# Attention on 8-column query tiles, its projections spread over four heads, and the keys' copies issued on ScalarE's queue

## The chip, the cores and the metric

One NeuronCore of one Trainium2 chip runs the whole program. TensorE (PE in the profile; its weight loads are PEld) multiplies into PSUM, VectorE (DVE) and ScalarE (ACT) do the elementwise work, GpSimd (POOL) casts some weights, and SyncE (SP) issues most DMAs. The metric is the device time of one execution in microseconds; lower is better. The time before is the median of three runs, 2376.87 us (2376.11 to 2376.95).

## The reference, cut to what matters

Two token streams, a prompt of 1024 tokens on a grid of 16 rows by 64 columns and a sample of 256 tokens on 4 by 64, go through two layers with the same weights. The change touches layer 0 alone: RMSNorm, four projections, attention in a clamped window of 8 rows by 16 columns with a learned bias, a gate, an output projection and the residual.

```python
proj = h @ w_in
q, k, v, g = jnp.split(proj, 4, axis=-1)
q = grid(q) * (NA_HEAD_DIM ** -0.5)
# per query row r: key rows rs..rs+7, key columns in a window of 16
s = jnp.einsum('bjqhd,bijkhd->bhjqik', q_r, k_s).astype(jnp.float32)
s = jnp.where(mask, s + bias, NEG_INF)
p = jax.nn.softmax(...)
o = jnp.einsum('bhjqik,bijkhd->bjqhd', p, v_s)
return (o * jax.nn.silu(g)) @ w_out
```

There are 16 heads of 64 channels. Everything is float32.

## The kernel before

Activations lie channel-major, 128 channels by 1280 tokens (1024 of the prompt, then 256 of the sample), and the prompt's tokens are sorted by grid column, so 128 tokens are 8 columns of 16 rows. Each projection is exact to float32 by three products of a high and a low part in fp32r: `proj` (line 1108) makes channel-major outputs in blocks of 512, 512 and 256 tokens, 24 matmuls a block; `proj_tokens` (line 1124) makes token-major strips of 128 tokens for V, 24 matmuls of 256 columns a strip.

Layer 0 runs over 16 heads. `qk_head(h)` projects queries and keys of a head, splits the keys into KH and KL and copies both from partitions 64 to 127 to partitions 0 to 63 by a DMA on SyncE's queue (lines 202 and 203). `g_pair(p)` makes the gate of two heads, `v_quad(q)` the values of four. `attention(h)` is a Python generator: each `yield n` says that n columns of projection should be streamed before it goes on, and the `Side` object steps it from `tick`, which every projection matmul calls. So the attention of head h is interleaved with the projections for later heads: `qk_head(h + 1)` beside every head, and in addition a whole `g_pair` beside every odd head and a whole `v_quad` beside every fourth. What is left of a head's attention at the end of this is drained. The framework's scheduler then sets the final order on each engine from this order of writing and the dependencies.

A head's prompt has four query tiles j of 16 columns. For a tile, two score blocks (`scores`, one for query rows 0 to 7, one for 8 to 15) of 128 queries by 384 keys: 12 key rows by a slab of 32 columns. Each is two matmuls (KH, then KL; lines 279 and 280), a sum with the bias and a minimum (line 224), Exp (line 225), a reciprocal and a scaling (lines 226 and 227) into a buffer P of 32 by 16 keys whose four unused rows hold zeros. `pv` then turns P with 8 TensorE transposes a tile (line 238), splits the turned block into ph and pl (ScalarE line 241, VectorE line 242) and multiplies both with the four strips of V that the slab covers, in 8 matmuls of 256 columns (line 254) into one PSUM tile O. Lines 259 to 261 take O out with the gate. The sample is a fifth tile: two score blocks of 256 keys (lines 299 and 300), 4 transposes, 4 products. The biases of a head come in three DMAs of 384 KB and one for the sample.

Q is stored with a permuted column order, so that the 128 queries of a score block lie together.

Of the kernel before, what the change touches and what calls it, by code (L numbers as in the profile page):

```python
# [19 lines left out]
NEG = -1e30  # L20
SLAB = [0, 8, 24, 32]
ROWS = [(0, 12), (4, 12)]
# [14 lines left out]
def layer0(ctx, tc, a, h1_out):  # L37
# [77 lines left out]
    def v_quad(q, side):  # L115
        nonlocal wv
        wv = load_v(tc, a, q)
        V = {}
        for s in range(10):
            side.until(lambda: done[4 * q - 1] > (0, 1, 1, 2, 3, 3, 3, 3, 4, 4)[s])  # L120
            V[s] = v_strip(s, token_major(s, side))
        return V

# [51 lines left out]
    with st:  # L175
# [5 lines left out]
        def qk_head(h, side=None):  # L181
# [4 lines left out]
            for b, (t0, n) in enumerate(BLK):  # L186
# [5 lines left out]
                if t0 < NP:  # L192
                    qv = Q[:, :NP].rearrange("p (g c r) -> p c g r", g=2, r=8)[:, t0 // 16:t0 // 16 + 32]
                    tq = t.rearrange("p (c g r) -> p c g r", g=2, r=8)
                else:
                    qv, tq = Q[:, c], t[:, :n]
                nc.scalar.activation(qv[0:64], tq[0:64], AF.Copy)
                nc.scalar.activation(KH[64:128, c], t[64:128, :n], AF.Copy, scale=0.125)
                nc.vector.tensor_sub(qv[64:128], tq[0:64], qv[0:64])
                nc.vector.scalar_tensor_tensor(KL[64:128, c], t[64:128, :n], 0.125, KH[64:128, c],  # L200
                                               op0=OP.mult, op1=OP.subtract)
            nc.sync.dma_start(KH[0:64, :].bitcast(F32), KH[64:128, :].bitcast(F32))
            nc.sync.dma_start(KL[0:64, :].bitcast(F32), KL[64:128, :].bitcast(F32))
            return Q, KH, KL

        def g_pair(p, side=None):
            wh, wl = load_w(tc, a, a["w_g"][p])
            G = []
            for b, (t0, n) in enumerate(BLK):
# [3 lines left out]
                proj(nc, ps, wh, wl, XH, XL, b, side)  # L213
                t = ap.tile([128, 512], F32, name="t", bufs=2)[:, :n]
                nc.vector.tensor_mul(t, ps, rb[:, t0:t0 + n])
                G.append(ap.tile([128, n], F32, name=f"G{b}"))
                nc.scalar.activation(G[b], t, AF.Tanh, scale=0.5)
                nc.vector.scalar_tensor_tensor(G[b], G[b], 1.0, t, op0=OP.add, op1=OP.mult)
            return G
# [9 lines left out]
        def pv(strips, hh, Od, Gv, t1v):  # L229

            O = ps_o.tile([128, 256], F32, name="O")
            ns = len(strips)

            def turned(s0):
                pt = ps_t.tile([128, 2, 256], F32, name="pt")
                for u in range(2):
                    for g in range(2):
                        nc.tensor.transpose(pt[:, u, 128 * g:128 * g + 128], strips[s0 + u][1][g], ident)  # L238
                ph = ap.tile([128, 2, 256], F32R, name="ph", bufs=2)
                pl = ap.tile([128, 2, 256], F32R, name="pl", bufs=2)  # L240
                nc.scalar.activation(ph, pt, AF.Copy)  # L241
                nc.vector.tensor_sub(pl, pt, ph)
                return ph, pl

            ts = []
            for s0 in range(0, ns, 2):
                ts.append(turned(s0))
                yield 800
            for s0 in range(0, ns, 2):
                ph, pl = ts[s0 // 2]  # L250
                for i, p in enumerate((ph, pl)):
                    for u in range(2):
                        v = strips[s0 + u][0][:, hh, :, :].rearrange("p a b -> p (a b)")
                        nc.tensor.matmul(O, v, p[:, u, :], start=(s0 + u + i == 0), stop=(s0 + u + i == ns))  # L254
                    yield 800
            b = 64 * (hh % 2)
            cc = 64 - b
            t1 = ap.tile([128, 256], F32, name="t1", bufs=2)
            nc.scalar.activation(t1[b:b + 64], O[cc:cc + 64], AF.Copy, scale=0.5)
            nc.vector.scalar_tensor_tensor(t1[b:b + 64], O[b:b + 64], 0.5, t1[b:b + 64], op0=OP.mult, op1=OP.add)  # L260
            nc.vector.tensor_mul(Od[b:b + 64], t1v(t1)[b:b + 64], Gv[b:b + 64])

        def attention(h, qkk, V, G, O):
            Q, KH, KL = qkk
            g3 = lambda t: t[:, :NP].rearrange("p (c r) -> p c r", r=16)
            g4 = lambda t, j: t[:, 256 * j:256 * j + 256].rearrange("p (c g r) -> p g c r", g=2, r=8)
            bts = {}

            def scores(j):
                if j != 2:  # L270
                    bts[j] = ap.tile([128, 768], F32, name="bias", bufs=2)
                    nc.sync.dma_start(bts[j], a["bias_p"][h, (0, 1, 1, 2)[j]])
                bt = bts[1 if j == 2 else j]
                s0 = SLAB[j]
                Pt = []
                for g, (r0, nr) in enumerate(ROWS):
                    S = ps_s.tile([128, 512], F32, name="S")[:, :nr * 32]
                    q = Q[:, 512 * g + 128 * j:512 * g + 128 * j + 128]
                    nc.tensor.matmul(S, q, g3(KH)[:, s0:s0 + 32, r0:r0 + nr], start=True, stop=False)
                    nc.tensor.matmul(S, q, g3(KL)[:, s0:s0 + 32, r0:r0 + nr], start=False, stop=True)  # L280
                    p = P[g][j % 2]
                    b = bt[:, 384 * g:384 * g + 384]
                    cr = lambda v: v.rearrange("p (c r) -> p c r", c=32)
                    softmax(cr(S), cr(b), p[:, :, r0:r0 + nr])
                    Pt.append(p)
# [1071 lines left out]
```

## Time and profile before

| what | value |
|---|---|
| median of three runs | 2376.87 us |
| the profiled execution's own time | 2384.96 us |
| its span, first to last instruction | 2383.2 us |
| mean granted TensorE clock | 0.971 |
| stretch of the heads' attention | about 57 to 707 us of the span |
| busy share of the span: PE, DVE, ACT, POOL | 95%, 70%, 51%, 23% |

Start times in the trace count from the span's first instruction. A matmul's duration there includes the time that it stands in the pipeline, so that two matmuls overlap: what one costs TensorE is the distance from its start to the start of the next one. The view by stretches gives the busy time of each engine and the count of its instructions between two moments; the granted clock in it is 1.00 at full speed.

### The profile page before, as it was taken

The numbers are of one execution on the slowest core, as the hardware profiler recorded it, in microseconds if no ns is written. First come the engines' busy times: TensorE is split into PE (matmuls) and PEld (weight loads), VectorE is DVE, ScalarE is ACT, GpSimd is POOL, SyncE is SP. The second block draws the span as 40 slices with busy tenths as digits, with TensorE's granted clock in tenths as the row PEclk, the third lists the DMA queues.
The fourth block names the chain that finished last, engine by engine and source line by source line (L and its number), as shares of the span: only waits on it lengthen the run. The fifth ranks groups of instructions, "written<-read, shape, count | busy, mean of one in ns | idle before, by whom it ended". The sixth has DMA issues, their size and how long they took to land.

```text
span 2383.2 us, 37349 instructions
## 1 busy us (share of the span) xinstructions
PE 2267.1 (95%) x13462; PEld 1967.4 (83%) x13462; DVE 1676.6 (70%) x3888; ACT 1213.0 (51%) x2742; POOL 544.1 (23%) x636
## 2 busy tenths in 40 slices
PE   8999999999999789999999999999999889999998
PEld 7889889889778678888989889898777777777887
DVE  5675774883783758578697786977588888886444
ACT  6553553563572543433444434443677777765233
POOL 2000101000120422222232222322544444420000
PEclk9999999999999899889999999998999999999999
DMA  5453443543556243333444433543533334347332
GB/s 173 119 125 86 118 119 92 130 106 97 139 164 197 67 108 102 77 102 108 112 115 115 129 99 112 115 116 103 135 95 110 115 108 114 105 152 249 105 105 86
DMA packets 150329, 281.34 MB, mean 118 GB/s; under 512 B 45824, under 2 KB 82688, under 8 KB 150144
## 3 DMA queue, kind: packets, MB, share of 16 engines
q1 hardware_dynamic: 137760, 233.86, 32.0%
q0 software_dynamic: 12384, 45.09, 10.6%
q8 instruction: 106, 1.74, 0.3%
q14 instruction: 79, 0.65, 0.1%
HBM read 203.54 MB, written 64.88 MB: 113 GB/s over the span
## 4 chain that ended last, share of the span: by engine, by line
PE 66%; DVE 21%; ACT 4%; DMA 4%; issue 4%; POOL 1%; SPq 0%; DVEq 0%; ACTq 0%; POOLq 0%
PE mm L1108 29%; PE mm L1124 11%; DVE acc L447 3%; PE O L254 3%; DVE tmp L562 3%; DVE X L564 3%; PE k L873 2%; PE k L864 2%; PE o L884 2%; PE pt L238 2%; PE u L839 2%; PE o L839 2%; PE m L610 1%; PE m L953 1%; PE S L280 1%
## 5 line engine op out<-in xcount | busy, mean ns | idle before, releaser
L1108 PE MATMUL mm<-xh,wh 128*128 128x512 f32 (+1 forms) x1536 | 556.7, 363 | 6.6 <-ACT wh L1060 5.9
L1108 PE MATMUL mm<-xh,wl 128*128 128x512 f32 (+1 forms) x1536 | 554.4, 361 | 6.4 <-DMA wl<-w_qkv 3.5
L1108 PE MATMUL mm<-xl,wh 128*128 128x512 f32 (+1 forms) x1536 | 559.7, 364 | 0.0
L1108 PEld LDWEIGHTS mm<-xh,wh 128*128 128x128 f32 x1536 | 293.0, 191 | 38.4 <-ACT wh L1060 6.4
L1108 PEld LDWEIGHTS mm<-xh,wl 128*128 128x128 f32 x1536 | 292.8, 191 | 37.9 <-DMA wl<-w_qkv 3.7
L1108 PEld LDWEIGHTS mm<-xl,wh 128*128 128x128 f32 x1536 | 293.1, 191 | 29.8 <-issue 0.5
L1124 PE MATMUL mm<-wh,xh 128*128 128x256 f32 x960 | 283.8, 296 | 5.1 <-DVE z L473 4.4
L1124 PE MATMUL mm<-wl,xh 128*128 128x256 f32 x960 | 284.0, 296 | 2.4 <-DMA wl<-w_z 1.9
L1124 PE MATMUL mm<-wh,xl 128*128 128x256 f32 x960 | 282.4, 294 | 0.3 <-POOL xl L66 0.3
L447 DVE SCALAR_TENSOR_TENSOR acc<-raw,cw,acc 128x1282 f32<-128x1282 f32 x128 | 201.1, 1571 | 46.8 <-ACT acc L445 45.1
L1124 PEld LDWEIGHTS mm<-wh,xh 128*128 128x128 f32 x960 | 188.9, 197 | 9.8 <-DVE z L473 4.8
L1124 PEld LDWEIGHTS mm<-wl,xh 128*128 128x128 f32 x960 | 188.9, 197 | 6.0 <-DMA wl<-w_z 2.2
L1124 PEld LDWEIGHTS mm<-wh,xl 128*128 128x128 f32 x960 | 189.0, 197 | 3.7 <-issue 2.0
L1060 ACT ACTIVATE wh<-wraw 128x1024 fp32r<-128x1024 f32 x94 | 98.8, 1056 | 141.9 <-PE mm L1108 81.0
L1058 POOL CAST wh<-wraw 128x1024 fp32r<-128x1024 f32 x30 | 31.4, 1048 | 471.5 <-PE mm L1108 373.2
L1108 PE MATMUL mm<-yh,wh 128*128 128x512 f32 (+1 forms) x384 | 135.7, 356 | 1.7 <-ACT yh L982 1.7
L1108 PE MATMUL mm<-yl,wh 128*128 128x512 f32 (+1 forms) x384 | 137.0, 358 | 0.1
L1108 PE MATMUL mm<-yh,wl 128*128 128x512 f32 (+1 forms) x384 | 136.4, 357 | 0.6 <-DVE wl L1062 0.6
L860 POOL TENSOR_TENSOR Al<-A,Ah 128x128 fp32r<-128x128 f32 x160 | 76.2, 482 | 174.2 <-ACT Ah L859 146.8
L1064 ACT ACTIVATE wl<-wraw 128x1024 fp32r<-128x1024 f32 x86 | 90.8, 1055 | 31.7 <-PE mm L1108 11.4
L450 ACT ACTIVATE th<-acc 128x1282 f32<-128x1282 f32 x32 | 40.9, 1277 | 129.3 <-DVE acc L447 129.3
L241 ACT ACTIVATE ph<-pt 128x512 fp32r<-128x512 f32 x144 | 84.3, 593 | 32.2 <-PE pt L238 31.3
(324 smaller groups left out, 5303.0 us busy)
## 6 DMA issues: line engine op xcount, KB each, us to landing
bias<-bias_p SPq DMA_DIRECT2D x48, 384.0 KB, 3.1
wraw<-w_qkv SPq DMA_DIRECT2D x32, 512.0 KB, 4.3
wl<-w_qkv POOLq DMA_DIRECT2D x32, 512.0 KB, 7.5
qkv_spill<-th SPq DMA_DIRECT2D x32, 512.0 KB, 2.6
wraw<-w_go SPq DMA_DIRECT2D x32, 512.0 KB, 3.7
z_spill<-z SPq DMA_DIRECT2D x80, 128.0 KB, 1.7
z<-z_spill SPq DMA_DIRECT2D x80, 128.0 KB, 2.1
wraw<-w_qk SPq DMA_DIRECT2D x16, 512.0 KB, 5.6
```

The costliest lines, as they stand in the source:

```text
L238: nc.tensor.transpose(pt[:, u, 128 * g:128 * g + 128], strips[s0 + u][1][g], ident)
L241: nc.scalar.activation(ph, pt, AF.Copy)
L254: nc.tensor.matmul(O, v, p[:, u, :], start=(s0 + u + i == 0), stop=(s0 + u + i == ns))
L447: nc.vector.scalar_tensor_tensor(acc, r[:, i:i + m], cw[:, f, i:i + 1], acc, op0=OP.mult, op1=OP.add)
L562: nc.vector.tensor_mul(tv, N[:, 0:c, c:c + 1].to_broadcast([128, c, n]), X[:, c:c + 1, c + 1:32].to_broadcast([128, c, n]))
L564: nc.vector.tensor_add(X[:, 0:c, c + 1:32], X[:, 0:c, c + 1:32], tv)
L839: self.tc.nc.tensor.matmul(ps, w[x], v[y], start=(first and i == 0), stop=(i == 2))
L860: nc.gpsimd.tensor_sub(As[d][1], A[:, d, c], As[d][0])
L1060: nc.scalar.activation(wh, raw, AF.Copy)
L1064: nc.scalar.activation(wl, raw, AF.Copy, scale=-1.0)
L1108: nc.tensor.matmul(ps, w[:, k, :], x[k][b], start=(k == 0 and i == 0), stop=(k == KD - 1 and i == 2))
L1124: nc.tensor.matmul(ps, x[k][b][:, cc], w[:, k % 4, :], start=(k == 0 and i == 0), stop=(k == KD - 1 and i == 2))
```

## The change

The query tile is now read as two blocks m of 8 columns by all 16 rows, which is how the tokens lie already. A block needs the keys of its own 8 columns and of the 8 on each side: three strips of 128 keys, two at the left and the right end of the grid (blocks 0 and 7). Scores are again 128 by 384, or 128 by 256 for the two end blocks, over plain slices. Two blocks still share one output tile: the two strips in the middle serve both of them (256 columns), the outer ones one each (an "edge", 128 columns). A first turned block holds the two middle strips, a second one the edges. The transposes for tile j now follow the products of tile j-1, instead of preceding the products of the same tile at once. All prompt biases of a head come in one DMA of 448 KB.

The gate's blocks and the strips of V are handed out in pieces: heads 0, 4, 8, ... get block 2 of the gate, six strips and `qk_head`, heads 1, 5, ... block 0 of the next gate and `qk_head`, heads 2, 6, ... blocks 1 and 2 and `qk_head`, heads 3, 7, ... two blocks of the next gate, four strips and `qk_head`. Delay and pace of the generator depend on h % 4. The two copies of the keys are issued by ScalarE.

```diff
-            nc.sync.dma_start(KH[0:64, :].bitcast(F32), KH[64:128, :].bitcast(F32))
-            nc.sync.dma_start(KL[0:64, :].bitcast(F32), KL[64:128, :].bitcast(F32))
+            nc.scalar.dma_start(KH[0:64, :].bitcast(F32), KH[64:128, :].bitcast(F32))
+            nc.scalar.dma_start(KL[0:64, :].bitcast(F32), KL[64:128, :].bitcast(F32))
...
+            for us in (units[:2], units[2:]):
+                if not us:
+                    break
                 pt = ps_t.tile([128, 2, 256], F32, name="pt")
...
+                for u, parts in enumerate(us):
+                    for s, q0, blocks in parts:
+                        for i, blk in enumerate(blocks):
+                            o = q0 + 128 * i
+                            nc.tensor.transpose(pt[:, u, o:o + 128], blk, ident)
...
+            order = [0, *range(2, len(units)), 1]
+            for i in range(2):
+                for u in order:
+                    p = ts[u // 2][i]
+                    for s, q0, blocks in units[u]:
+                        qs = slice(q0, q0 + 128 * len(blocks))
+                        v = V[s][:, hh, :, :].rearrange("p a b -> p (a b)")
+                        nc.tensor.matmul(O[:, qs], v, p[:, u % 2, qs], start=(i == 0 and u == 0),
+                                         stop=(i == 1 and u == 1))
+                yield 1600
...
+                for m in (2 * p, 2 * p + 1):
+                    k0, k1 = max(m - 1, 0), min(m + 2, 8)
+                    n = 128 * (k1 - k0)
...
+                    nc.tensor.matmul(S, q, KH[:, 128 * k0:128 * k1], start=True, stop=False)
+                    nc.tensor.matmul(S, q, KL[:, 128 * k0:128 * k1], start=False, stop=True)
...
+            for j in range(5):
+                units = yield from (scores(j) if j < 4 else scores_s())
+                if last:
+                    yield from products(*last)
+                else:
+                    yield 3200
+                ts = yield from turned(units)
+                last = j, units, ts
...
-            side.add(attention(h, qkk, V, G, O), 8000)
+            side.add(attention(h, qkk, V, G, O), (2000, 2000, 4000, 4000)[h % 4], (1.8, 0.95, 1.2, 1.75)[h % 4])
+            side.tick(0)
+            p, q = (h + 1) // 2, (h + 1) // 4
+            if h % 2 == 0:
+                g_pair(p, G, [b for b in range(3 if h % 4 == 0 else 2) if b not in G], side)
+                v_quad(q, V, [s for s in range(8) if s not in V], side)
             if h < 15:
-                side.tick(0)
                 qkk = qk_head(h + 1, side)
...
+            if h % 2 == 0:
+                g_pair(p, G, [b for b in range(3) if b not in G], side)
+                v_quad(q, V, [s for s in range(10) if s not in V], side)
+            elif h < 15:
+                nG = {}
+                g_pair(p, nG, [0], side)
                 if h % 4 == 3:
-                    V = v_quad((h + 1) // 4, side)
+                    nV = {}
+                    v_quad(q, nV, range(4), side)
+                    g_pair(p, nG, [1], side)
```

What this does to TensorE is best seen at one tile. In the program before, this stands on TensorE at the second tile of head 3 (ph and pl are the high and low part of the turned block, V_465 and so on the strips of V, mm the projection that is interleaved):

```order
L238 MATMUL pt<-ident,P_869 128x128
L1108 MATMUL mm<-xh_1_108,wh 128x512
L1108 MATMUL mm<-xl_1_132,wh 128x512
L254 MATMUL O<-ph,V_465 128x256
L254 MATMUL O<-ph,V_468 128x256
L1108 MATMUL mm<-xh_1_108,wl 128x512
L1108 MATMUL mm<-xh_1_111,wh 128x512
L254 MATMUL O<-pl,V_465 128x256
L254 MATMUL O<-pl,V_468 128x256
```

In the changed program this stands on TensorE at the products of the same tile of the same head, with the end of a projection ahead and the next tile's transposes behind:

```order
L1129 MATMUL mm<-xl_2_136,wh 128x256
L1129 MATMUL mm<-xh_2_112,wl 128x256
L259 MATMUL O<-ph,V_468 128x256
L259 MATMUL O<-ph,V_465 128x128
L259 MATMUL O<-ph,V_608 128x128
L259 MATMUL O<-ph,V_520 128x256
L259 MATMUL O<-pl,V_468 128x256
L259 MATMUL O<-pl,V_465 128x128
L259 MATMUL O<-pl,V_608 128x128
L259 MATMUL O<-pl,V_520 128x256
L239 MATMUL pt<-ident,P 128x128
```

Before, two projection matmuls stood between the last transpose and the first product, and products with ph and pl went in pairs; now the transposes of a tile are a score step ahead of its products, which stand together, and two of the four products of each part have 128 columns.

On ScalarE the two copies now stand behind the last piece of the keys, here in head 5's `qk_head` (V are the strips of values, t the step that takes O out):

```order
L1085 ACTIVATE wl<-wraw 128x1024
L190 ACTIVATE Q<-t 64x256
L191 ACTIVATE KH<-t 64x256
L195 DMA KH<-KH 64x1280
L196 DMA KL<-KL 64x1280
L110 ACTIVATE V_2944<-mm,rs 128x4x64
L110 ACTIVATE V_2972<-mm,rs 128x4x64
L1085 ACTIVATE wl<-wraw 128x1024
L265 ACTIVATE t_2980<-O 64x256
```

The second of them waits for VectorE, which makes KL, and everything behind it on ScalarE stands in line.

More of the change, by code (lines that the diff above doesn't have):

```diff
@@ L239, in turned @@
                 ph = ap.tile([128, 2, 256], F32R, name="ph", bufs=2)
                 pl = ap.tile([128, 2, 256], F32R, name="pl", bufs=2)
[L241 to L247, printed above, removed]
-                yield 800
[L249 to L255, printed above, removed]
+                n = 0
@@ L267, in attention @@
[L267 to L285, printed above, removed]
+            bt = ap.tile([128, 896], F32, name="bias", bufs=2)
@@ L286, in scores @@
                     yield 800
[L287 to L290 removed]
+                m = 2 * p
+                edge = [(s, 128 * i, [own[s, m + i]]) for s, i in ((m - 1, 0), (m + 2, 1)) if (s, m + i) in own]
+                return [[(s, 0, [own[s, m], own[s, m + 1]])] for s in (m, m + 1)] + [edge]
```

129 lines of the change are left out of this document (64 added, 65 removed).

## The prediction

> **What bounds the kernel now.** I read the page first, then the heads' part by stretches, then single matmuls in the timeline, then the waits.
>
> ```profile
> span 2383.2 us, 37349 instructions
> PE 2267.1 (95%) x13462; PEld 1967.4 (83%) x13462; DVE 1676.6 (70%) x3888; ACT 1213.0 (51%) x2742; POOL 544.1 (23%) x636
> ```
>
> TensorE is busy nearly throughout, so removed matmuls count, but a pipelined matmul's busy time says little. The view by stretches is therefore cut at the ends of successive `qk_head` projections: each stretch holds one head's attention and the projections beside it.
>
> ```profile
> core 0: us, PE busy (x) PEld busy (x) DVE busy (x) ACT busy (x) POOL busy (x), PEclk, DMA share, GB/s
> 99.41:127.07 27.66, 27.50 (x168) 22.91 (x167) 24.43 (x69) 17.90 (x43) 2.36 (x3) 1.00 0.45 115
> 127.07:167.67 40.60, 40.09 (x236) 33.93 (x234) 28.01 (x75) 20.03 (x46) 3.35 (x4) 1.00 0.48 121
> 195.34:265.10 69.76, 69.12 (x475) 62.74 (x474) 32.88 (x85) 26.65 (x58) 7.33 (x8) 1.00 0.41 101
> 431.62:460.31 28.69, 27.72 (x169) 23.05 (x167) 24.45 (x69) 17.90 (x43) 2.37 (x3) 1.00 0.43 111
> 626.45:673.92 47.47, 43.49 (x242) 36.32 (x241) 34.28 (x81) 31.28 (x68) 14.31 (x12) 0.96 0.69 200
> ```
>
> Three kinds alternate: short ones with `qk_head` alone (seven, 27.65 to 28.69 us), middle ones with a gate pair (three, 40.58 to 40.87), long ones with V too (three, 69.71 to 69.91), and a last, odd one of 47.47. How much of each is work follows from the spacing of single matmuls.
>
> ```profile
> 300.79 0.40 PE L254 MATMUL O<-pl,V 128*128 128x256 f32 x2
> 301.02 0.39 PE L1108 MATMUL mm<-xh,wl 128*128 128x512 f32 x1
> 301.25 0.39 PE L1108 MATMUL mm<-xh,wh 128*128 128x512 f32 x1
> 301.49 0.60 PE L238 MATMUL pt<-ident,Ps 128*128 128x128 f32 x4
> 301.84 0.48 PE L1108 MATMUL mm<-xl,wh 128*128 128x512 f32 x1
> 302.15 0.39 PE L1108 MATMUL mm<-xh,wl 128*128 128x512 f32 x1
> ...
> 648.25 0.34 PE L279 MATMUL S<-KH,Q 128*128 128x384 f32 x1
> 648.43 0.34 PE L280 MATMUL S<-KL,Q 128*128 128x384 f32 x1
> 648.60 0.40 PE L1108 MATMUL mm<-xl,wh 128*128 128x512 f32 x1
> ```
>
> Start to start: two 256-column products 0.23 us, so 0.12 each; a 512-column matmul 0.23; a 384-column score (648.60 - 648.25) / 2 = 0.175. Four transposes take 0.35, and the matmul behind them 0.31 where 0.23 is usual: 0.43 / 4 = 0.108 each. A short stretch then holds 48 x 0.23 + 24 x 0.12 of `qk_head` (13.9) and one head's attention: 36 transposes 3.9, 36 products 4.3, 16 x 0.175 + 4 x 0.12 of scores 3.3, together 11.5. That is 25.4 of 27.66: 2.3 us are waits. A middle stretch holds twice the projections, 27.8 + 11.5 = 39.3 of 40.60 (1.3 waits), a long one 240 x 0.12 = 28.8 more, 68.1 of 69.76 (1.7). So TensorE is the limit in the middle and long ones; in the short ones VectorE is busy 24.43 of 27.66 us (88%) and TensorE waits more. All waits: five short ones 2.3 each and two 3.2, middle 4.2, long 5.1, and 47.47 - 39.3 = 8.2 in the last: 35 us.
>
> ```profile
> PEld O L254 <- DVE pl L242: 16.9, 62, 0.5
> PEld O L254 <- ACT ph L241: 16.7, 61, 0.5
> PEld S L299 <- DVE mx L224: 7.9, 14, 0.9
> PE pt L238 <- DVE P L227: 4.0, 5, 2.9
> ```
>
> These rows of the waits (total, times, longest, in 60 to 720 us) say where: weight loads of the products waiting for ph and pl, 123 times, the sample's score waiting for the PSUM block that VectorE still reads, and one transpose waiting 2.9 us. The 2.9 is dearer than it looks:
>
> ```profile
> 652.50:656.90 4.40, 1.54 (x9) 0.94 (x8) 2.22 (x8) 2.55 (x7) 0.09 (x2) 1.00 1.04 329
> 656.90:660.40 3.50, 3.50 (x15) 3.02 (x13) 3.47 (x7) 3.43 (x8) 1.26 (x1) 0.51 0.90 326
> ```
>
> Behind the gap the granted clock is 0.51 for 3.5 us, another 1.7 us lost.
>
> **The change part by part.** *Matmuls removed and added.* Transposes go from 36 to 26 a head (the tiles have 5, 6, 6, 5 in place of 8, the sample 4): 160 fewer x 0.108 = 17.3 us. Products: 576 of 256 columns become 320, and 192 edge products of 128 columns are new; 256 x 0.12 = 30.7 us go. Scores: 64 of 128 are cut from 384 to 256 columns for KH and KL together, 64 x (0.175 - 0.12) = 3.5 us.
>
> What an edge product costs, the trace doesn't show: no fp32r matmul in it has 128 columns. From below it is half of a 256-column product, 0.06 us, if only columns count. From above it is a whole fp32 product of that size:
>
> ```profile
> 1704.96 0.38 PE L797 MATMUL t<-qT,kT 128*128 128x128 f32 x2
> L797 PE MATMUL t<-qT,kT x160: 270/275/579, 1669.3 to 2088.2; 128*128 128x128 f32 x160
> ```
>
> These are 80 products in 160 records, two passes each; two records take 0.38 us, with the second alone 0.27, so they start 0.11 apart and a product costs 0.22. The nearest row is the transpose: 128 columns with a weight load of its own for each, 0.108. I take 0.11: 192 x 0.11 = 21.1 us come in (ends 11.5 and 42.2). The sum on TensorE is 17.3 + 30.7 + 3.5 - 21.1 = **30.4 us less**, 1.9 a head, on the path because TensorE is the limit.
>
> The Trainium skill, "TensorE: Matmul & The Clock Gate", section "Back-to-back issue gap", gives about 81 ns a matmul for a sustained stream of weight load and matmul at 128 columns. By that the edges would cost 15.6 us, and the sum would be 5.5 better; the nearest row, at 0.108 us, speaks against it.
>
> *Waits.* The projections beside a head become, with 2.9 us for a V strip or the gate's block 2, 5.5 for a 512-token block of the gate, 13.9 for `qk_head` and 9.6 for attention: 43.8, 29.0, 31.9 and 46.1 us for h % 4 = 0 to 3. The short stretch of 25.4 us of work, where VectorE sets the pace, is left only at head 0. VectorE's own work falls too:
>
> ```profile
> L242 DVE TENSOR_TENSOR pl<-pt,ph 128x512 fp32r<-128x512 f32 x144 | 97.7, 683 | 3.4 <-ACT ph L241 1.9
> L260 DVE SCALAR_TENSOR_TENSOR t<-O,t 64x256 f32<-64x256 f32 x80 | 33.7, 422 | 26.0 <-ACT t L259 25.0
> ```
>
> 64 of the 144 splits shrink from 512 columns to 256 or 128, from 683 ns to about 422 or less (the 256-column row): some 17 us over the layer, an estimate. Against it, beside h % 4 = 1 there are 29.0 us of TensorE work and about 24 of VectorE, still 83%. I give the four kinds the waits of the nearest old ones, 1.7, 2.3, 1.3 and 1.7, 1.75 on average: 23 us for the thirteen stretches that now lose 27, and 1.5 in place of 8.2 for the last, where the order has no transpose left so close behind its scores: **11 us less**. From below, nothing is gained: the transposes now follow their scores at a shorter distance than before. From above, all 35 go, 24 more.
>
> *Copies on ScalarE's queue.* One head's:
>
> ```profile
> 433.09 0.41 ACT L198 ACTIVATE KH<-t 64x256 fp32r<-64x256 f32 x1
> 433.52 1.06 ACT L1064 ACTIVATE wl<-wraw 128x1024 fp32r<-128x1024 f32 x1
> 433.53 0.47 SPq L202 DMA_DIRECT2D KH<-KH  x1
> 434.36 0.42 DVE L200 SCALAR_TENSOR_TENSOR KL<-t,KH 64x256 fp32r<-64x256 f32 x1
> 434.84 0.74 SPq L203 DMA_DIRECT2D KL<-KL  x1
> 441.29 0.45 PE L280 MATMUL S<-KL,Q 128*128 128x384 f32 x1 [0.80 <-DMA KL<-KL]
> ...
> SPq L202 <- ACT KH L198: 23.8, 15, 1.8
> SPq L203 <- DVE KL L200: 10.9, 14, 0.8
> ```
>
> SyncE already waits for both producers, so the copies can't start earlier elsewhere: no gain. ScalarE pays: from 433.50 it issues KH, waits for KL until 434.8 and issues that until 435.6, 2.1 us a head in which it worked before (the wl of 1.06, then t and ph). At 17.90 of 27.66 us busy it has the room; queued behind are V, wl, t and ph, and TensorE's products wait for ph. I take 0, as the transposes now stand a score step ahead of their products; the other end is 15 x 2.1 = 32 us.
>
> *Biases.* 16 DMAs of 448 KB for 48 of 384: SyncE only, 0 (nothing on TensorE waits for them now; without that cover a landing of 3 us a head).
>
> The sum: 30.4 + 11 = 41.4. The profiled execution took 2384.96, so 2343.6; it is 8.1 us above the median of the runs, and the forecast is **2335 us**.
>
> **The rivals.** *Edges at the full fp32 price.* 192 x (0.22 - 0.11) = 21 us are given back: 2356. For it: the only 128-column products in the trace cost that. Against it: those need two passes, and fp32r matmuls of 256 to 512 columns need one.
>
> *ScalarE's stop shows.* If ph and Exp come 2.1 us late and about half of it is uncovered, 15 x 1 = 15 us: 2350. For it: 61 waits for ph already. Against it: the greater distance to the products.
>
> *No balance.* The scheduler sets the final order; if VectorE's chain still decides, only the matmuls count: 2346.
>
> *Copies too late, and slower.* The scores of a head now begin 2000 to 4000 columns after their copies instead of 8000. KL already held a score for 0.80 us at 441.29. Should it hold TensorE for 2.9 us at the start of the 12 heads whose scores stand close behind their copies, the clock would halve as at 656.90: 12 x (2.9 + 1.7) = 55 us, 2390. It decides from 41.4 / 12 = 3.5 us a head. Against it: in the order, other TensorE work of some 8 us, counted at the spacings above, stands between the last key matmul and those scores, as it did before in half the heads.
>
> On such gaps the same page of the Trainium skill, section "The HAM clock gate (the "warmup" mystery)", says that the clock halves after an idle window of about 3.4 us. The one case here had a gap of 2.9, so shorter gaps can be enough.
>
> **How the numbers follow.** Forecast 0.50, edges dear 0.18, ScalarE 0.14, no balance 0.10, copies late 0.08 (of which 0.05 slower and 0.03 within 0.2%, about what a measurement of this kernel can tell from no change). Faster is 0.92. The range runs from 2314 (edges at 0.06 gain 10, half of the remaining waits 12) to 2358 (edges dear, a few us of ScalarE's stop); all the unknowns together, at their ends, would give 2302 and 2399.
>
> **What would show it.** A short stretch's attention should hold 92 - 14 = 78 or so matmuls; edge products should start 0.11 apart; the waits of the products' weight loads should fall from 33.6 us to under 20; the scores' waits for KL should stay under 1 us a head; no stretch of the heads should show a granted clock under 1. It would be wrong if 0.2 us stands between edge products, if ScalarE's copies are what ph waits for, or if the time saved in layer 0 comes back in later stages through clock drops.

## The result, and the profile after

The changed kernel took 2404.98 us (median of four runs, 2400.87 to 2414.32) against 2376.91 for the kernel before: a ratio of 1.0121, 95% interval 1.0101 to 1.0142. It is **slower by 1.2%**, where the forecast was 2335 us in a range of 2314 to 2358. The rival "copies too late, and slower", at 2390, came closest.

The page of the profiled execution (2400.87 us) begins:

```profile
span 2399.1 us, 36727 instructions
PE 2237.3 (93%) x13238; PEld 1950.1 (81%) x13238; DVE 1661.8 (69%) x3888; ACT 1192.3 (50%) x2742; POOL 543.7 (23%) x632
```

The 224 matmul records that the change takes away are gone (13462 to 13238: 160 transposes and 64 products), and TensorE has 30 us less busy time in a longer span. Where the time went is seen at one mark that both programs have: the first residual addition behind the output projection (its line's instructions: duration min/median/max in ns, first and last start), in the kernel before

```profile
L368 DVE TENSOR_TENSOR p<-mm,xres x16: 1033/1083/1109, 707.3 to 779.5; 128x512 f32<-128x512 f32 x16
```

and after:

```profile
L389 DVE TENSOR_TENSOR p<-mm,xres x16: 1077/1083/1117, 727.9 to 800.2; 128x512 f32<-128x512 f32 x16
```

The heads end **20.6 us later** (707.3 to 727.9); all of the loss of these two executions is there, and behind the mark the program even takes 4.7 us less. (The two profiled executions, 2384.96 and 2400.87 us, lie 16 us apart, the medians 28.) The heads' stretch as one window, first before, then after (columns: length, busy time and count by engine, granted TensorE clock, DMA share, GB/s):

```profile
57.00:745.00 688.00, 676.23 (x4123) 580.84 (x4122) 455.24 (x1192) 353.40 (x771) 75.15 (x77) 1.00 0.48 125
```

```profile
57.00:745.00 688.00, 631.06 (x3797) 552.93 (x3796) 430.97 (x1182) 325.51 (x761) 72.40 (x73) 0.96 0.40 99
```

Two things are new: TensorE is busy 45 us less in the same window, and its clock fell from 1.00 to 0.96 on average, up to 688 x 0.04 = 27 us of lost speed. What TensorE waited for, in 57 to 740 us (total, times, longest):

```profile
PE S L282 <- DMA KH<-KH: 23.9, 8, 5.4
PE mm L1129 <- DMA wl<-w_qk: 14.6, 3, 5.4
PE mm L1145 <- DMA wl<-w_v: 8.0, 3, 3.1
PE pt L239 <- DVE mx L220: 3.9, 5, 1.3
PE pt L239 <- DVE P L221: 2.9, 6, 1.1
PE S L283 <- DMA KL<-KL: 1.8, 3, 1.0
PEld O L259 <- DVE pl L244: 2.6, 9, 0.5
PEld O L259 <- ACT ph L243: 2.5, 8, 0.5
```

Scores wait 25.7 us for the copies (before: 1.5 us, all for KL), projections 22.6 us for weights (before: none). The chain of work that ended last runs through these DMAs now; three of its longest pieces (start, us, what):

```profile
343.51 8.91 DMA KH<-KH
...
442.87 9.92 DMA wl<-w_qk
...
481.25 9.67 DMA KL<-KL
```

A KH copy is on the chain for as long as it takes from issue to landing, and that time more than doubled. The rows of DMA issues (KB each, median us to landing), before

```profile
KH<-KH SPq DMA_DIRECT2D x16, 320.0 KB, 3.2
KL<-KL SPq DMA_DIRECT2D x16, 320.0 KB, 4.9
```

and after:

```profile
KH<-KH ACTq DMA_DIRECT2D x16, 320.0 KB, 7.5
KL<-KL ACTq DMA_DIRECT2D x16, 320.0 KB, 8.4
```

The timeline of one head shows what stands around such a copy (start, duration, engine or queue, what):

```profile
341.05 1.06 ACT L1085 ACTIVATE wl<-wraw 128x1024 fp32r<-128x1024 f32 x1 [0.48 <-PE mm L1129]
343.51 0.47 ACTq L195 DMA_DIRECT2D KH<-KH  x1
344.40 0.47 ACTq L196 DMA_DIRECT2D KL<-KL  x1
...
342.20 6.61 SPq L1075 DMA_DIRECT2D wraw<-w_v  x2
...
342.41 0.86 POOL L1086 DMA_DIRECT2D wl<-w_g  x1 [0.24 <-ACT wl L1085]
...
352.46 0.58 PE L282 MATMUL S<-KH,Q 128*128 128x256 f32 x1 [5.37 <-DMA KH<-KH]
```

At 341.05 ScalarE writes the next weight's `wl` (the negated copy, onto which the accumulating load then adds); that frees the one `wraw` buffer, and so two weight loads of 512 KB (342.20 and 342.41) leave 1.1 to 1.3 us ahead of KH (343.51), which lands at 352.42. In the head of the kernel before that the prediction shows, the same instruction (433.52) stands right behind KH's rounding (433.09), the copy leaves at 433.53, and the loads follow it. The gap has its second price, as the windows of it and of the time behind it say:

```profile
346.50:351.90 5.40, 0.59 (x3) 0.17 (x1) 0.14 (x1) 1.06 (x1) 1.90 (x2) 0.91 1.04 216
351.90:355.40 3.50, 2.94 (x8) 2.46 (x9) 0.00 (x0) 0.00 (x0) 0.00 (x0) 0.50 1.04 243
```

TensorE does next to nothing for 5.4 us and then runs at half clock for 3.5.

### The profile page after: what moved, and what is told of

Read it like the earlier page. It is cut to its first block, busy times and chain, and to the rows that moved or that the text cites. A ratio compares the mean times of both kernels' runs of the same rounds, so it can differ in the third digit from the quotient of the medians.

```text
span 2399.1 us, 36727 instructions
## 1 busy us (share of the span) xinstructions
PE 2237.3 (93%) x13238; PEld 1950.1 (81%) x13238; DVE 1661.8 (69%) x3888; ACT 1192.3 (50%) x2742; POOL 543.7 (23%) x632
## 3 DMA queue, kind: packets, MB, share of 16 engines
q0 software_dynamic: 12384, 45.09, 10.5%
## 4 chain that ended last, share of the span: by engine, by line
PE 59%; DVE 22%; DMA 8%; ACT 5%; issue 3%; POOL 1%; SPq 0%; DVEq 0%; ACTq 0%; POOLq 0%
PE mm L1129 27%; PE mm L1145 11%; DVE acc L468 3%; DVE tmp L583 3%; DVE X L585 3%; PE k L894 2%; PE k L885 2%; PE u L860 2%; PE o L905 2%; PE o L860 2%; DMA KH<-KH 2%; DMA wl<-w_qk 2%; PE O L259 1%; PE pt L239 1%; DMA KL<-KL 1%
## 5 line engine op out<-in xcount | busy, mean ns | idle before, releaser
L1129 PE MATMUL mm<-xh,wl 128*128 128x512 f32 (+1 forms) x1536 | 560.0, 365 | 20.0 <-DMA wl<-w_qk 15.2
L468 DVE SCALAR_TENSOR_TENSOR acc<-raw,cw,acc 128x1282 f32<-128x1282 f32 x128 | 201.2, 1572 | 46.8 <-ACT acc L466 45.0
L219 ACT ACTIVATE P<-P,mx 128x384 f32<-128x384 f32 (+1 forms) x128 | 74.9, 586 | 100.9 <-DVE mx L218 100.4
L218 DVE CUSTOM_DVE_ANT_0 P<-S,bias 128x384 f32<-128x384 f32 (+1 forms) x128 | 64.7, 518 | 76.7 <-PE S L283 75.7
```

What stands on the lines that cost most here:

```text
L218: nc.vector.tensor_tensor_reduce(Pv, S, bias, -1.0, 3e38, OP.add, OP.min, mx[:, 0:1])
L219: nc.scalar.activation(Pv, Pv, AF.Exp, scale=-1.0, bias=mx[:, 0:1], accum_out=mx[:, 1:2])
L468: nc.vector.scalar_tensor_tensor(acc, r[:, i:i + m], cw[:, f, i:i + 1], acc, op0=OP.mult, op1=OP.add)
L1129: nc.tensor.matmul(ps, w[:, k, :], x[k][b], start=(k == 0 and i == 0), stop=(k == KD - 1 and i == 2))
```

## The experiments

Each run is set against the kernel before on its own chip (the medians of the kernel before are 2376.50 to 2379.60 on them), so medians of rows from different chips compare to about 3 us. "Mark" is the start of the first residual addition, "copies" and "weights" are TensorE's waits for KH and KL and for wl in 57 to 740 us, each from one profiled execution.

| run | what it is | us | ratio (95%) | mark | copies | weights |
|---|---|---|---|---|---|---|
| before | | 2376.91 | 1 | 707.3 | 1.5 | 0 |
| after | the change | 2404.98 | 1.0121 (1.0101-1.0142) | 727.9 | 25.7 | 22.6 |
| copies_sync | after, copies on SyncE | 2396.81 | 1.0075 (1.0047-1.0103) | 719.8 | 22.7 | 18.1 |
| before_act | before, copies on ScalarE | 2395.62 | 1.0064 (1.0043-1.0086) | 721.8 | 10.5 | 0 |
| tiles_only | new tiles alone | 2376.09 | 0.9978 (0.9960-0.9995) | 706.6 | 18.8 | 0 |
| late_scores | after, attention starts at 8000 | 2388.72 | 1.0047 (1.0026-1.0067) | 716.0 | 17.8 | 12.7 |
| sub_after | after, wl by subtraction | 2380.58 | 1.0015 (0.9999-1.0032) | 702.2 | 14.6 | 0 |
| sub_tiles | tiles_only, wl by subtraction | 2389.52 | 1.0044 (1.0027-1.0060) | 720.8 | 0 | 0 |
| sub_before | before, wl by subtraction | 2403.41 | 1.0103 (1.0084-1.0122) | 732.7 | 0 | 0 |
| v89 | after, V strips 8, 9 first | 2412.50 | 1.0143 (1.0122-1.0163) | 740.8 | 40.0 | 9.0 |
| split_after | after, copies by block | 2354.80 | 0.9928 (0.9903-0.9953) | 682.5 | 0 | 17.0 |
| split_tiles | tiles_only, copies by block | 2348.69 | 0.9888 (0.9865-0.9910) | 677.1 | 0 | 0 |
| split_before | before, copies by block | 2375.34 | 0.9997 (0.9987-1.0006) | 704.9 | 0 | 0 |
| split_late | late_scores, by block on SyncE | 2354.49 | 0.9916 (0.9888-0.9944) | 682.5 | 0 | 7.1 |
| split_sync | split_after on SyncE | 2348.61 | 0.9882 (0.9866-0.9898) | 672.9 | 0 | 9.4 |
| split_v89_act | split_after and v89 | 2346.81 | 0.9866 (0.9850-0.9883) | 667.6 | 0 | 6.2 |
| split_v89 | the same on SyncE | 2340.38 | 0.9850 (0.9832-0.9867) | 662.9 | 0 | 0 |
| hold_tiles | tiles_only, wl held behind KL | 2354.74 | 0.9894 (0.9869-0.9919) | 684.1 | 0 | 0 |
| hold_after | after, wl held behind KL | 2392.12 | 1.0050 (1.0031-1.0069) | 716.6 | 16.3 | 23.3 |

### One part at a time

The queue alone, on the changed kernel and (with `nc.sync` to `nc.scalar`) on the kernel before:

```diff
-            nc.scalar.dma_start(KH[0:64, :].bitcast(F32), KH[64:128, :].bitcast(F32))
-            nc.scalar.dma_start(KL[0:64, :].bitcast(F32), KL[64:128, :].bitcast(F32))
+            nc.sync.dma_start(KH[0:64, :].bitcast(F32), KH[64:128, :].bitcast(F32))
+            nc.sync.dma_start(KL[0:64, :].bitcast(F32), KL[64:128, :].bitcast(F32))
```

> The changed kernel with the keys' two copies issued on SyncE's queue again, nothing else changed. Theory A (the copies are late because weight loads issued just ahead of them occupy the same DMA engines; the queue does not matter): TensorE still waits about 20 to 30 us for KH or KL, 2398 to 2410 us. Theory B (ScalarE's own queue makes them late): the 25 us of waits for KH and most of their clock drops go, about 2365 to 2375 us. The waits for wl of w_qk and w_v (23 us) stay under both.

> The kernel before with only the two copies moved to ScalarE's queue. Theory A: the loads stand where they stood, KH lands 3 to 4 us after its issue, within 5 us of before (2372 to 2382). Theory B: KH lands 7 us or more after its issue in the heads whose scores stand 8 us behind, and the time grows by 15 us or more.

Measured: back on SyncE the copies are hardly earlier (median 7.5 us to landing on either queue, 22.7 us of waits), and the time falls by 8 us of the 28 lost (1.0121 to 1.0075; the intervals just meet), to 1 us under theory A's range. So the loss in the change is not mainly the queue's. But on the kernel before, the queue alone cost 16 us, more than theory A allowed and as much as theory B had asked for, by a way that neither had named: ScalarE's order changes with it. At every second head `wl` now runs 4.2 us (at the last 2.6) ahead of the copy and KH lands in 6.9 to 8.7 us, at the others still in 3.2 to 3.9 (but for the first, late in the kernel before too). TensorE pays at KL, and at those others: there a load of `wraw` that left 2.7 to 2.8 us behind KL now leaves 0.1 to 0.2 us ahead of it, as SyncE is no longer held by the copies:

```profile
PE S L280 <- DMA KL<-KL: 10.5, 7, 3.9
```

The new tiles alone take the old allotment of projections, delay 8000, pace 1 and copies on SyncE; the late start keeps all of the change but the delay:

```diff
-            side.add(attention(h, qkk, V, G, O), (2000, 2000, 4000, 4000)[h % 4], (1.8, 0.95, 1.2, 1.75)[h % 4])
+            side.add(attention(h, qkk, V, G, O), 8000, (1.8, 0.95, 1.2, 1.75)[h % 4])
```

> The changed kernel with its new tiles, but with the projections, the delay of 8000 and the pace of the kernel before and the copies on SyncE's queue. Theory C (the loss comes from the new spreading of the projections, which moves the weight loads and holds V's weights over two heads; the tiles themselves save what their matmuls cost): about 25 to 35 us faster than before, 2340 to 2352 us, waits for KH and wl under 5 us in all. If the tiles themselves bring the waits (the transposes closer behind their scores), 2370 us or more.

> The changed kernel with the delay of 8000 columns ahead of every head's attention in place of 2000 and 4000. If TensorE waits for copies only because the scores stand too close behind them: the 25 us for KH fall below 10 and some clock drops go, 2375 to 2390 us; the waits for wl stay. If the copies are late by what is issued, at whatever distance: within 5 us of the changed kernel.

Measured: `tiles_only` comes within 0.4% of the kernel before, where theory C had 2340 to 2352. Its waits:

```profile
PE pt L239 <- DVE P L221: 14.6, 26, 3.6
PE S L282 <- DMA KH<-KH: 12.1, 7, 2.3
PE S L283 <- DMA KL<-KL: 6.7, 7, 1.6
```

KH lands late here too (median 8.1 us), on SyncE, with the old order of the projections. The 14.6 us for P are new with the tiles (4.0 before), as the other branch of that expectation had it, but they are not what hides the gain: they stay (14.1) in `split_tiles` below, which has it. The early start makes the late copies dearer (`late_scores` is 16 us better than the change, with 12.9 us of waits for KH where under 10 were expected), but isn't their cause: KH lands in 8.7 us there.

### Fewer bytes, and another order of V

If the copies are late because weight loads share the DMA engines with them, a kernel without the second, accumulating load should have them in time:

```diff
-    if eng:
-        eng.tensor_sub(wl, raw, wh)
+    if eng or a.get("hi"):
+        (eng or nc.gpsimd).tensor_sub(wl, raw, wh)
```

> The changed kernel, but in the attention stage the low half of each weight (wl) is worked out on GpSimd as raw minus high half, in place of ScalarE's negated copy and a second, accumulating load of 512 KB from DRAM; values unchanged. In the changed kernel's trace every KH copy that is issued 0.5 to 2.5 us behind a pair of weight loads (wraw and the accumulating wl) lands 6.9 to 9.5 us after its issue, every one with no weight load within 20 us ahead of it lands in 3.2 to 3.3. Theory A (the copies share the 16 DMA engines with the weight loads issued just ahead of them): half of the load's bytes are gone, and the other half waits for the subtraction of about 2.7 us, so KH lands 3.2 to 5.5 us after its issue, the waits of the scores for KH and KL, about 51 us by both rows of KH before, fall below 15, the half-clock time falls from 51 to under 30 us, and the time is 2365 to 2388 us. Rival B (ScalarE's own queue is slow, or the copies slow each other): KH stays at 7 us or more, and the time stays at 2395 to 2405. Rival D (weights that come later through a slower GpSimd subtraction hold the projections): KH lands early but waits of the projections for wl grow by as much, 2395 to 2410.

> The run tiles_only (the new query tiles with the old order of projections and the copies on SyncE) with the same subtraction in place of the accumulating load. Theory A: KH from 7.8 on the average to 3.2 to 5.5 us, the 21 us of waits for KH and KL and most of the 13 us lost at half clock go, 2345 to 2362 us against 2376; the 18 us of waits of the transposes for P stay. Rival B: no change, 2370 to 2380. This is also the test of whether the tiles' own saving of some 30 us is there when the copies are in time.

> Control: the kernel before with the same subtraction. There KH already lands in 3.2 us and TensorE waits little for copies or weights, so by theory A the time moves by less than 6 us either way (2371 to 2383). If the subtraction itself is what makes a kernel faster, this one gains as much as the two others.

> The changed kernel with V strips 8 and 9 made ahead of the next Q and K projection in heads 0, 4, 8 and 12, not behind it, so that the w_v buffers come free one projection sooner. If the waits for wl of w_qk (14.6 us in 3, and the half clock behind each) come from buffers held by these two strips, they go: 15 to 22 us less, 2380 to 2388. If they come from the load's own length on shared DMA engines, they move to another load and the time stays within 5 us of the changed kernel's.

Measured: the landing did what theory A said (KH median 3.3 us in `sub_after`; 3.2 in `sub_tiles`, which has no wait for copies left), and the time of `sub_after`, 2380.6, lies in its range. But `sub_tiles` came over 27 us above its range and lost 13 us to `tiles_only`, and the control lost 25 us. The subtraction has a price of its own, on VectorE. In `sub_before` and in the kernel before, the scaling of P, 60 to 700 us:

```profile
L227 DVE TENSOR_SCALAR P<-P,mx 128x384 f32<-128x384 f32 x118 | 77.0, 653 | 1.2
```

```profile
L227 DVE TENSOR_SCALAR P<-P,mx 128x384 f32<-128x384 f32 x128 | 55.7, 436 | 1.3
```

One of the long ones, beside the subtraction on GpSimd, in `sub_before`:

```profile
201.83 1.90 DVE L227 TENSOR_SCALAR P<-P,mx 128x384 f32<-128x384 f32 x1
...
200.94 2.57 POOL L1062 TENSOR_TENSOR wl<-wraw,wh 128x1024 fp32r<-128x1024 f32 x1
```

GpSimd is at it from 200.94 to 203.51, and VectorE's scaling, begun at 201.83, ends at 203.73 in place of 202.24. Seventeen of the 118 are that long, up to 2.58 us; sixteen of them meet a subtraction, and all sixteen end 0.21 to 0.22 us behind its end. The Trainium skill, "SBUF — State Buffer", section "SBUF: two separate sides", has VectorE and GpSimd share a port pair as "an exclusive lock, not a bandwidth split"; the 1.90 us agree. In `sub_tiles` it is another step of VectorE that meets the subtraction, the one that makes the last piece of Q; in `sub_tiles` and in `tiles_only`:

```profile
L192 DVE TENSOR_TENSOR Q<-t,Q 64x256 fp32r<-64x256 f32 x16 | 31.3, 1957 | 0.9 <-ACT Q L190 0.5
```

```profile
L192 DVE TENSOR_TENSOR Q<-t,Q 64x256 fp32r<-64x256 f32 x16 | 6.7, 419 | 1.4 <-ACT Q L190 1.0
```

So these three runs tell of the copies' landing, not of what it is worth. `v89` traded one wait for another: no wait for w_qk, but 35.9 us for KH in 11 (8 before that edit): the copies land as late as in the change, median 7.5 us, and more scores meet it. Its 2412.5 us is above both forecasts for it.

### The copies block by block

The scores' wait for the copies can be taken away without touching a weight:

```diff
                 nc.vector.scalar_tensor_tensor(KL[64:128, c], t[64:128, :n], 0.125, KH[64:128, c],
                                                op0=OP.mult, op1=OP.subtract)
-            nc.scalar.dma_start(KH[0:64, :].bitcast(F32), KH[64:128, :].bitcast(F32))
-            nc.scalar.dma_start(KL[0:64, :].bitcast(F32), KL[64:128, :].bitcast(F32))
+                nc.scalar.dma_start(KH[0:64, c].bitcast(F32), KH[64:128, c].bitcast(F32))
+                nc.scalar.dma_start(KL[0:64, c].bitcast(F32), KL[64:128, c].bitcast(F32))
```

> The changed kernel with the copies of KH and KL issued block by block (512, 512 and 256 columns, each as soon as its block is made, still on ScalarE's queue) in place of one copy each at the end of the projection. The first scores then wait for the first block's copies, which are issued a whole block ahead (5.5 us of matmuls or more), and the weight loads stay where they are. Theory A (what costs is that the copies stand behind the weight loads and the scores wait for all of them): the waits for KH (25.2 us in 8) and KL (2.6) go, with the half clock behind them some 8 to 14 us, and the time is 2362 to 2378. The waits for weights (15.1 and 8.7 us) and the half clock behind those stay. Rival E (the copies only hid the next wait: the transposes for P on VectorE, as in sub_tiles): the waits of transposes and scores for VectorE grow by 15 us or more and the time is 2380 to 2395. Rival F (six issues a head on ScalarE's queue cost more than the waits): 2395 or more.

> The run tiles_only with the copies block by block on SyncE. This shows the new query tiles' own worth with the copies in time. Theory A: 13.3 and 8.0 us of waits for KH and KL and most of 13 us at half clock go: 2345 to 2360 against 2376. Rival E: the waits for P and mx grow instead from 18 to 35 us or more, and the time is 2366 to 2380.

> Control: the kernel before with the copies block by block on SyncE. Its scores wait 1.8 us for KL in all, so by theory A nothing is to be gained: 2370 to 2382. A gain of over 10 us would say that the split does something else than bring the copies in time.

> The changed kernel with the copies block by block on SyncE, and with each head's attention starting 8000 columns into the projections as before in place of 2000 to 4000. If the early start was only harmful because the copies were late, this is no faster than split_after (2362 to 2380); if the early start has a price of its own (waits for VectorE at the start of a head), it is faster by 5 us or more.

Measured: no wait for KH or KL is left in any of the four. The change gains 50 us by it (`split_after` 2354.8), the tiles 27 (`split_tiles` 2348.7), the kernel before nothing (0.9997, interval 0.9987 to 1.0006). Theory A held, beyond its numbers for `split_after`; rivals E and F fell, and so did the control's alternative. The early start has no price of its own: `split_late` equals `split_after`, and is no faster than `split_sync` (2348.6, below), from which only the start sets it apart. Not every piece lands early; in `split_tiles`:

```profile
KH<-KH SPq DMA_DIRECT2D x32, 128.0 KB, 2.2
KH<-KH SPq DMA_DIRECT2D x16, 64.0 KB, 6.7
```

The last pieces, the smallest, have two weight loads just ahead of them at 14 heads and land in 6.3 to 7.1 us there, in 1.9 at the two others. So a fifth of the bytes is late as well; but the first scores don't need that piece, and none waits for it.

### What is left: weights, and the queue

> The changed kernel with the copies block by block, on SyncE (split_after has them on ScalarE). With the copies in time the queue is the only difference. If ScalarE's queue has a price of its own (the six issues a head, or the weight loads that SyncE then sends off earlier), this is faster than split_after's 2354.8 by 4 to 10 us; if the whole price of the queue was that the copies came late, the two are within 4 us (2350 to 2358).

> split_after with V strips 8 and 9 ahead of the Q and K projection in heads 4, 8 and 12, as in v89. v89 took the 14.6 us of waits for w_qk away, but the waits for KH rose from 23.9 to 35.9 us and the time did not fall. If that rise was the same cause (copies behind the weight loads, all scores waiting for all of them), then with the copies block by block the wait for w_qk goes and nothing takes its place: 15 us of the 688 at half clock go with it, 2338 to 2350. If the projections' order has a price of its own on VectorE, waits of transposes and scores for VectorE rise by 8 us or more and the time stays at 2350 to 2360.

> The same with the copies on SyncE: the candidate that keeps the balance and the tiles with neither wait. As split_v89_act, and apart from it by as much as split_sync from split_after: 2333 to 2350. split_tiles (2348.7) is the mark: below 2345 the balanced order is worth something once its waits are gone; at 2345 to 2352 it is worth nothing over the old order.

Measured: with the copies in time ScalarE's queue still costs 6 us, in both pairs (2354.8 to 2348.6, with intervals that don't meet, and 2346.8 to 2340.4, whose intervals overlap a little). The place is ScalarE's order again, in `split_after`

```profile
184.65 0.41 ACT L191 ACTIVATE KH<-t 64x256 fp32r<-64x256 f32 x1
...
185.09 0.47 ACTq L195 DMA_DIRECT2D KH<-KH  x1
185.90 0.47 ACTq L196 DMA_DIRECT2D KL<-KL  x1
186.42 0.87 ACT L243 ACTIVATE ph<-pt 128x512 fp32r<-128x512 f32 x2 [1.09 <-DVE t L266]
187.32 1.07 ACT L1085 ACTIVATE wl<-wraw 128x1024 fp32r<-128x1024 f32 x1
```

against `split_sync`:

```profile
182.72 0.41 ACT L191 ACTIVATE KH<-t 64x256 fp32r<-64x256 f32 x1
183.04 0.36 ACT L265 ACTIVATE t<-O 64x256 f32<-64x256 f32 x1
183.43 1.06 ACT L1085 ACTIVATE wl<-wraw 128x1024 fp32r<-128x1024 f32 x1
```

`wl` follows KH's rounding by 0.7 us with the copies on SyncE and by 2.7 on ScalarE, where the two issues and a `ph` stand between; the accumulating load of w_v is issued as much later, and the projection waits for it 6.7 us in three on ScalarE, 0.2 on SyncE. V strips 8 and 9 ahead of the projection are worth 8 us on either queue (w_qk's waits of 10.3 and 9.2 us go). With both, `split_v89` has this left:

```profile
PE S L301 <- DVE mx L218: 6.4, 8, 1.8
PE pt L239 <- DVE mx L220: 2.5, 4, 0.8
PE pt L239 <- DVE P L221: 2.4, 4, 1.1
PE S L282 <- DVE mx L218: 2.3, 2, 2.1
```

and a granted clock of 1.00 over the heads. At 2340.38 us it beats both kernels (0.9850, 0.9832 to 0.9867).

### Why the copies came behind the loads

The two `hold` kernels bind the one load that reuses the buffers of a head's w_qk to that head's keys, and change nothing else:

```diff
+            z = ap.tile([128, 1], F32, name="z", bufs=4)
+            nc.vector.memset(z[0:64], -1.0)
+            nc.vector.tensor_scalar(z[64:128], KL[64:128, T - 1:T].bitcast(F32), 0.0, -1.0, op0=OP.mult, op1=OP.add)
...
-        nc.scalar.activation(wl, raw, AF.Copy, scale=-1.0)
+        nc.scalar.activation(wl, raw, AF.Copy, scale=z)
```

> The run tiles_only (copies whole, on SyncE) in which the one weight load that reuses the buffers of a head's w_qk is held back: ScalarE's negated copy wl is scaled by a column z = -1 that VectorE makes from the last column of KL, so that it can't run ahead of the head's keys. In every run so far where ScalarE's wl stands behind KH's rounding (0.0 us after the KH copy's issue, or later) the copy landed in 3.1 to 4.7 us, in every one where it stood 1.8 to 4.2 us ahead of it in 6.9 to 9.6. If the place of that one instruction is what makes the copies late: KH lands in 3.1 to 4.7 us in all heads but the first, the waits for KH and KL (13.3 and 8.0 us) fall below 4, and the time comes to split_tiles's 2348.7, within 8 us. If the later weights are needed by then, waits for wl appear and the time stays above 2360.

> The changed kernel itself with the same hold, copies whole and on ScalarE. Here some other weight loads (of w_v and w_g) still come just ahead of a copy at one or two heads in four, and the 22.6 us of waits for weights stay or grow as the loads start 2 to 4 us later. So KH lands in 3 to 5 us at most heads, its waits fall from 23.9 to under 10, and the time falls by 10 to 35 us, to 2370 to 2395. If it does not fall at all, the held weights cost as much as the copies gained.

Measured in `hold_tiles`:

```profile
KH<-KH SPq DMA_DIRECT2D x16, 320.0 KB, 3.2
KL<-KL SPq DMA_DIRECT2D x16, 320.0 KB, 3.9
```

All sixteen KH copies land in 3.1 to 3.3 us, no score waits for one, and the time falls from 2376.1 to 2354.7. That settles it for the tiles: the copies were late because ScalarE's `wl` stood ahead of the keys and set two loads free. In `hold_after` the copies that nothing else precedes land in 3.2 to 4.3 us, those behind another load still in 7.5 to 9.1; 16.3 us of waits stay (under 10 were expected), and the time falls by 13 us. So in the change itself the held load is one of several that come ahead of a copy.

What made the scheduler place `wl` earlier is open. It does so in `tiles_only`, so neither the queue nor the balance is needed, though the queue alone does it at every second head of `before_act`; the tiles and the merged bias DMAs were not tried apart.

## Why the prediction was wrong

**Matmuls, 30.4 us less: right.** `split_tiles`, which has no wait for copies or weights, passes the mark 30.2 us ahead of the kernel before (677.1 and 707.3). That the two agree to 0.2 us is luck: between these two traces matmuls wait 10 us more for P (14.1 and 4.0), and the products' weight loads 19 us less for ph and pl (14.3 and 33.6). The prediction's "64 of 128" shortened scores are 64 of 256, KH and KL together; its 3.5 us stand. The edges cost what I took, 0.11 us: in the timeline after, a group of two 256-column and two edge products

```profile
246.75 0.62 PE L259 MATMUL O<-ph,V 128*128 128x256 f32 x4
247.21 0.28 PE L1145 MATMUL mm<-wl,xh 128*128 128x256 f32 x1
```

takes 0.46 us, 0.24 of them for the two wide ones. The rival of dear edges fell with this.

**Waits, 11 us less: not in the kernel as it is written.** The products' weight loads do wait only 5.1 us for ph and pl (33.6 before, under 20 forecast). But with the copies in time and on SyncE, the balanced order is worth nothing (`split_tiles` 2348.7, `split_sync` 2348.6; at the mark of the profiled executions 4.2 us). V strips 8 and 9 behind `qk_head` hold both w_v buffers, so that the next w_qk load starts late: 14.6 us of waits in the change, 9.2 in `split_sync`. With the two strips moved it is worth 8.3 us (`split_v89`; 14.2 at the mark), near the 11. The prediction counted the projections' matmuls by head and not when their weights' buffers come free.

**Copies on ScalarE's queue, 0: the step that failed.** "SyncE already waits for both producers, so the copies can't start earlier elsewhere" is true, and beside the point. The sum has no term for when the copies land: it left their landing as it was (3.2 us for KH), when that depended on ScalarE's `wl` standing behind KH; the row that says so (433.52, right behind KH at 433.09) was in the prediction's own fence. ScalarE's order in the changed program, shown ahead of the prediction for head 5, begins with a `wl` that stands ahead of Q and KH; the two were not set against each other, nor were the loads that this `wl` sets free. In the change KH lands in 7.5 us, and scores wait 25.7 us for copies with the half clock behind that. The whole miss can be taken back step by step: with the copies by block 2405.0 becomes 2354.8, with these on SyncE 2348.6, and with the strips of V moved, which belongs to the term of the waits, 2340.4, 5 us above the forecast. The Trainium skill, "DMA: Bandwidth & Descriptors", section "Issuing engines are not separate DMA queues", says that DMAs of all issuing engines run on the same 16 DMA engines and interleave; that KH lands in 7.5 us behind two loads on either queue agrees.

**The rival that came closest** had the right wait and half of the mechanism. It let scores wait for copies, with the clock halved behind the gap; but it made the copies late because the scores had moved close, and not because the copies land later. With the scores as far off as before, they are still waited for (17.8 us in `late_scores`, 18.8 in `tiles_only`). That its 2390 lies near is partly luck: its price of 2.9 us at 12 heads was 35 us of waits; measured are 25.7, in 11. Its clock term, 1.7 us a gap, was 20; the windows bound it by 27, for all gaps. And it lacked the weights' 22.6. What was held against it, 8 us of other work between the keys and the scores, is too short: in the head shown KH is issued 2.5 us behind the end of the last key matmul (343.51; ScalarE's `wl`, which that end released, begins at 341.05) and lands 8.9 us later. The sum at the mark does not close exactly: 30 us gained by matmuls and 46.8 lost to new waits make 17 us, and up to 24 of clock (half clock stood for 51.2 us of the heads, 3.4 before), of which a part falls into the waits, would make 41; 20.6 are measured.

**ScalarE's stop**, the rival at 15 us, exists at another place: not ph but `wl` comes late, for 6 us.

**Biases, 0:** nothing on TensorE waits for them after; whether three DMAs in SyncE's queue held the loads back before is part of what is open.

## What to carry to other kernels

A DMA's landing time depended here on what was in flight beside it: before a copy close to the critical path is moved, or the code around it reordered, look up in the trace what frees the buffers of the large loads, and whether that instruction stays behind the copy. A transfer that feeds the next stage can be cut and sent in pieces as they are made: in the changed kernel that gained 50 us where holding one load back gained 13, while with the new tiles alone the two did about the same (0.9888 and 0.9894). Price a gap on TensorE with the half clock behind it, and take waits of weights by the order in which their buffers come free.

## What the runs showed of the hardware

- The clock halves for 3.4 or 6.8 us behind gaps that are shorter than that. In the traces of seventeen of these kernels (all but the two `hold` ones), half clock began within a gap of TensorE in the heads, or up to 1.7 us behind it, at 36 of 37 gaps of 3.1 us or more, 34 of 50 between 2.0 and 3.1 us, 7 of 12 between 1.6 and 2.0, and 5 of 37 between 1.2 and 1.6 us.
- A copy of 320 KB between partitions lands in 3.1 to 4.8 us with no weight load issued just ahead (once, among seven loads of `xl`, in 6.3), and in 6.9 to 9.6 with two weight loads of 512 KB issued 0.5 to 3.1 us ahead of it; of the pieces, those of 128 KB land in 2.2 to 2.4 us (medians), and those of 64 KB in `split_tiles` in 1.9, or in 6.3 to 7.1 behind two such loads.
- A subtraction of 128 by 1024 on GpSimd held VectorE's scaling of P for up to 2.2 us (2.58 in place of 0.41); the scaling then ended 0.21 to 0.22 us behind the subtraction's end.
